# A perceptron's second product by Strassen's algorithm, in four groups of its inner dimension

## The chip, the cores and the metric

The kernel runs on one core of one Trainium2 chip. The metric is device time in microseconds for one execution of the whole program; lower is better. TensorE multiplies matrices into PSUM, which has eight banks of 128 x 512 numbers of 4 bytes here; VectorE, ScalarE and GpSimd do element by element work on SBUF and PSUM; SyncE (SP) issues transfers from DRAM.

## The reference, cut to what matters

The program is three layers over 512 tokens of width 1024: two mixer layers with a context of 256 tokens, and a third block with four mixers, a projection and a perceptron. Only the perceptron at the very end is touched. `x2` is the residual, 512 x 1024; with `h` its normalised copy and no biases:

```
hidden = square(relu(h @ w_mlp1))      # 512 x 1024 by 1024 x 4096
out    = x2 + hidden @ w_mlp2          # 512 x 4096 by 4096 x 1024
```

## The kernel before, in words

All large products are made with numbers split in two: `split` (537) casts a float32 tile to the float32r form (`hi`) and subtracts to get the rest (`lo`). `mm3` (757) then adds three matmuls in a PSUM bank: hi by hi, hi by lo, lo by hi. One matmul takes a 128 x 128 stationary operand and 512 moving columns.

Weights come in units of 128 x 1024 float32 numbers (512 KB). `wemit_raw` (719) issues the transfer of a unit into a tile `raw` on SP's queue, `wfill` (728) splits it into `whi` and `wlo` and keeps some units ahead, `wnext` (753) hands out the next one. Each filler of a list (`block2_fill`, 2496) names its units in order, so that the following stage's weights can be fetched and split during the present one.

The program is written out once in Python by a planner. Stages ("fillers") are generators that run one after another; side work is coroutines with a priority of their own, started with `spawn`. A `yield` names what the next instructions need, and `turn` (649) resumes whatever is ready by estimated times. The engine for an elementwise operation marked "*" is chosen by `best` (481): of the engines allowed, the one whose estimated queue end plus the estimated cost of this operation is earliest. The costs per column are

```
eng = (self.best(n, A=0.95, V=1.1) if self.in_psum(out, in_) else self.best(n, A=0.95, V=0.62, G=1.05)).lower()
eng = "v" if self.in_psum(out, a, b) else self.best(self.cols(out), V=1.1, G=2.0).lower()
```

for casts and for operations of two tensors (A is ScalarE, V VectorE, G GpSimd); each engine runs its instructions in the order in which they were written. SBUF tiles are placed by a plan made from their lifetimes in a first pass; `cap` (200000 bytes per partition) and `capw` (194000) limit how far ahead weights and tiles are made.

The perceptron has two rounds, each over 2048 of the 4096 hidden columns. `g_mlp1` (2321) makes 16 hidden tiles `m` of 128 columns, stored with the hidden dimension on partitions: `g_fm` (766) does 24 matmuls for a tile, ScalarE applies relu into `rl`, and a coroutine `co_hid` (2313) squares and splits it into two `hid` tiles. `g_mlp2` (2355) then makes the second product with `hid` stationary and the weights moving: for each half `c` of 512 output columns, eight weight units `u`, four token tiles `t` of 128, 6 matmuls for each (`u`, `t`), in four banks. After the last unit VectorE adds each bank to `x2` (tile name `z` in the trace); in the last round the tiles are then stored to `out`. In the last half the last two units are taken together tile by tile, so that the additions and stores spread.

Of the kernel before, what the change touches and what calls it, by code (L numbers as in the profile page):

```python
# [11 lines left out]
F32R = mybir.dt.float32r  # L12
U8 = mybir.dt.uint8
AF = mybir.ActivationFunctionType
# [4 lines left out]
D, S, CL = 1024, 512, 256  # L19
# [309 lines left out]
class Mem:  # L329
# [11 lines left out]
    def new(self, shape, dt=F32, tag="t"):  # L341
        size = int(np.prod(shape[1:])) * (1 if dt == U8 else 4)
        g = -(-size // self.G)
        i = self.plan[self.count] if self.plan is not None else (self.count * 67) % (self.n - 300)
        h = self.nc.alloc_sbuf_tensor_at(f"{tag}_{self.count}", list(shape), dt, offset=self.base + i * self.G)
        self.log.append([g, None])
        self.live += g
        self.peak = max(self.peak, self.live)
        self.curve.append((self.live, tag))
        self.count += 1  # L350
        return Tl(h, self.count - 1, g)
# [106 lines left out]
class K:  # L458
# [304 lines left out]
    def new_bank(self, n=1):  # L763
        return self.P.new(n, self.est)

    def g_fm(self, parts, evac):

        yield (self.after("h", "h0"),)
        w = self.wnext()
        hi, lo = (x.rearrange("p (k c) -> p k c", k=8) for x in w)  # L770
        yield w
        for i, (hh, hl, n) in enumerate(parts):
            yield (self.bank(), hh[:, 7], hl[:, 7])
            ps = self.new_bank()
            for k in range(8):
                self.mm3(ps[:, :n], hi[:, k], lo[:, k], hh[:, k], hl[:, k], k == 0, k == 7)
                if k % 2 and k < 7:
                    yield ()
            evac(i, ps)
            self.P.free(ps)  # L780
        self.M.free(*w)
# [158 lines left out]
    def w_ada(self, l, js, part=False):  # L940
        n = 2 if part else 4
        return [(self.I[f"wada{l}"][j * n + u], 1024, "raw") for j in js for u in range(n)]

    def w(self, name, idx):
        ap = self.I[name]
        return [(ap[i], ap.shape[2], "w") for i in idx]
# [1363 lines left out]
        for a in mix:  # L2310
            M.free(*a)

    def co_hid(self, r, hi, lo):
        M = self.M
        yield (r,)
        self.mul("*", r.f, r.f, r.f)
        yield (r,)
        self.split(hi.f, lo.f, r.f)
        M.free(r)

    def g_mlp1(self, first):
        M = self.M
        self.hid = []

        def evac(m, ps, o=0, n=S, r=None):
            r = r or M.new([128, S], tag="rl")
            self.act(r[:, o:o + n], ps[:, :n], AF.Relu)
            if o + n == S:
                hi, lo = M.new([128, S], F32R, "hid"), M.new([128, S], F32R, "hid")
                self.hid.append((hi, lo))  # L2330
                self.spawn("hid", self.co_hid(r, hi, lo), 0)
            return r
        m0 = 0
        if first:
            m0 = 3
            ws = [self.wnext() for _ in range(m0)]
            rs = {}
            for o in (0, 256):
                for t in range(o // 128, o // 128 + 2):
                    yield (self.after(("h", t)),)  # L2340
                for m in range(m0):
                    hi, lo = (x.rearrange("p (k c) -> p k c", k=8) for x in ws[m])
                    yield (hi, lo, self.bank())
                    ps = self.new_bank()
                    for k in range(8):
                        yield (self.hl[0][:, k, o:o + 256], self.hl[1][:, k, o:o + 256])
                        self.mm3(ps[:, :256], hi[:, k], lo[:, k], self.hl[0][:, k, o:o + 256], self.hl[1][:, k, o:o + 256], k == 0, k == 7)
                    rs[m] = evac(m, ps, o, 256, rs.get(m))
                    self.P.free(ps)
                    if o:  # L2350
                        M.free(*ws[m])
        for m in range(m0, 16):
            yield from self.g_fm([(self.hl[0].f, self.hl[1].f, S)], evac)

    def g_mlp2(self, last):
        nc, M, P = self.nc, self.M, self.P
        hid = self.hid
        for c in range(2):
            for _ in range(4):
                yield (self.until(lambda: self.P.used.count(False) >= 4),)  # L2360
            ps = [self.new_bank() for _ in range(4)]
            tail = 2 if last and c == 1 else 0

            def part(w, u, t):
                hi, lo = (x.rearrange("p (k c) -> p k c", k=2) for x in w)
                for kk in range(2):
                    k = 2 * u + kk
                    hh, hl = hid[k]
                    self.mm3(ps[t][:, :], hh[:, t * 128:(t + 1) * 128], hl[:, t * 128:(t + 1) * 128], hi[:, kk], lo[:, kk], k == 0, k == 15)

            def evac(t):
                x = self.x2[t][:, c * 512:(c + 1) * 512]
                self.add("v", x, x, ps[t][:, :])
                P.free(ps[t])
                if last:
                    (nc.sync if t % 2 else nc.scalar).dma_start(self.out[t * 128:(t + 1) * 128, c * 512:(c + 1) * 512], x)
            for u in range(8 - tail):
                w = self.wnext()
                if c == 0 and u == 7:
                    yield (self.after("hid"),)  # L2380
                yield (*w, hid[2 * u + 1][1])
                for t in range(4):
                    part(w, u, t)
                    yield ()
                M.free(*w)
            if tail:
                ws = [self.wnext() for _ in range(tail)]
                for t in range(4):
                    for i in range(tail):
                        part(ws[i], 8 - tail + i, t)  # L2390
                    evac(t)
                    yield ()
            else:
                for t in range(4):
                    evac(t)
        for a in hid:
            M.free(*a)

    def g_block2(self):
        M, I = self.M, self.I  # L2400
# [95 lines left out]
    def block2_fill(self):  # L2496
        w = self.w
        F = lambda name, g, u=(): Filler(name, g, u, gate=True)
        gates = []
        for m in range(8):  # L2500
            gates += w("wbr", [m]) + w("wgate", [4 * m + n for n in (0, 2, 3)])
        f = [F("block2", self.g_block2),
             F("n1", self.g_nsa_in, w("w2b", range(4)) + w("w2a", range(4))),
             F("convs", self.g_convs, w("w2f", (0, 2, 1, 3, 4, 6, 8, 5, 7, 9))),
             F("n2", self.g_nsa_in2, w("w2c", range(4)) + w("w2d", range(4))),
             F("gb", self.g_gateb, w("wgate", [4 * m + 1 for m in range(8)])),
             F("g", self.g_gates, gates),
             F("mix", self.g_mix, w("wbrb", range(2))),
             F("out2", self.g_out2, w("wout2", range(8)))]
        for r in range(2):  # L2510
            f.append(F(f"mlp{r}", lambda r=r: self.g_mlp1(r == 0), w("wm1", range(16 * r, 16 * r + 16))))
            f.append(F(f"mlp{r}o", lambda r=r: self.g_mlp2(r == 1), w("wm2", range(16 * r, 16 * r + 16))))
        return f


# [1 line left out]
           cap=200000, capw=194000, early=(0, 0),  # L2517
# [51 lines left out]
```

## Time and profile before

| | |
|---|---|
| median of 3 runs | 1953.08 us (1951.28 to 1953.52) |
| profiled execution | 1951.59 us, span 1949.9 us |
| mean granted TensorE clock | 0.982 of full speed |
| TensorE busy | 1831.2 us |
| VectorE / ScalarE / GpSimd busy | 1185.8 / 610.7 / 484.9 us |

The span runs from the first to the last instruction; the execution's own time has 1.7 us around it. TensorE matmuls are pipelined, so a matmul's own duration (389 ns for 512 columns) is longer than the distance between two of them. Almost every instruction carries line 282, that of the planner's recorder; the names of tiles tell them apart. A clock of 1.00 is 2.4 GHz and of 0.50 is 1.2 GHz.

### The profile page before, as it was taken

How to read it: one execution, taken by the hardware profiler on the slowest of the kernel's cores; microseconds unless marked ns; L12 is line 12 of the kernel's file. 1: busy time of each engine (PE TensorE's matmuls, PEld its weight loads, DVE VectorE, ACT ScalarE, POOL GpSimd, SP SyncE). 2: the span in 40 equal slices, each digit the busy share in tenths (PEclk: the TensorE clock that was granted, in tenths of full speed). 3: DMA queues.
4: the chain of work that ended last, by engine and by line, in shares of the span. 5: the costliest groups of instructions: out<-in, count | busy, mean ns of one | idle time of the engine just before them, and what ended most of it. 6: DMA issues, size and time to landing. Idle time of an engine off the chain costs nothing.

```text
span 1949.9 us, 28333 instructions
## 1 busy us (share of the span) xinstructions
PE 1831.2 (94%) x11374; PEld 1520.5 (78%) x11374; DVE 1185.8 (61%) x2072; ACT 610.7 (31%) x1281; POOL 484.9 (25%) x402
## 2 busy tenths in 40 slices
PE   6898889998999999899999899899999999999999
PEld 3688778777688788686887787778788788888887
DVE  2648686564757748766476879874632766445542
ACT  2335544553320246444152321343422211000100
POOL 1313232113422314324314453431211320000000
PEclk9999999999999999999999899999999999999999
DMA  9101001231233201003123222212232222222221
GB/s 362 66 11 45 1 12 45 88 117 68 98 119 120 95 23 38 29 12 125 47 76 132 94 87 71 71 52 70 93 100 96 98 87 87 97 98 97 84 93 61
DMA packets 45378, 159.19 MB, mean 82 GB/s; under 512 B 5040, under 2 KB 5552, under 8 KB 44992
## 3 DMA queue, kind: packets, MB, share of 16 engines
q1 hardware_dynamic: 42224, 148.54, 22.0%
q10 hardware_dynamic: 3024, 8.85, 1.2%
q8 instruction: 89, 1.46, 0.3%
q14 instruction: 41, 0.34, 0.1%
HBM read 152.12 MB, written 5.26 MB: 81 GB/s over the span
## 4 chain that ended last, share of the span: by engine, by line
PE 59%; DVE 14%; POOL 6%; issue 6%; ACT 3%; DMA 1%; SPq 0%; POOLq 0%; DVEq 0%; ACTq 0%
PE banks L282 59%; DVE cacc L282 2%; POOL t L282 2%; DVE sm L282 2%; DVE t L282 1%; DVE wlo L282 1%; ACT p L282 1%; DVE z L282 1%; POOL wlo L282 1%; DVE h L282 1%; DVE p L282 1%; DVE gt L282 1%; POOL yo L282 1%; POOL kh L282 1%; DMA raw<-win 0%
## 5 line engine op out<-in xcount | busy, mean ns | idle before, releaser
L282 PE MATMUL banks<-h,whi 128*128 128x512 f32 (+1 forms) x1968 | 578.6, 378 | 6.2 <-POOL h L282 1.9
L282 PEld LDWEIGHTS banks<-h,whi 128*128 128x128 f32 x1968 | 352.4, 191 | 69.5 <-issue 2.5
L282 PE MATMUL banks<-h,wlo 128*128 128x512 f32 (+1 forms) x984 | 367.1, 373 | 0.8 <-POOL wlo L282 0.8
L282 PE MATMUL banks<-whi,h 128*128 128x256 f32 (+3 forms) x1344 | 340.0, 335 | 15.1 <-DVE h L282 7.9
L282 DVE TENSOR_TENSOR wlo<-raw,whi 128x1024 fp32r<-128x1024 f32 (+1 forms) x169 | 223.6, 1328 | 115.5 <-PE banks L282 69.3
L282 PEld LDWEIGHTS banks<-whi,h 128*128 128x128 f32 x1344 | 237.9, 194 | 42.8 <-DVE h L282 9.5
L282 PE MATMUL banks<-wlo,h 128*128 128x256 f32 (+3 forms) x672 | 221.3, 330 | 11.0 <-DVE wlo L282 8.2
L282 POOL TENSOR_TENSOR wlo<-raw,whi 128x1024 fp32r<-128x1024 f32 (+2 forms) x47 | 116.1, 2470 | 447.9 <-DMA out<-z 299.8
L282 PEld LDWEIGHTS banks<-h,wlo 128*128 128x128 f32 x984 | 187.0, 190 | 35.7 <-issue 1.7
L282 DVE TENSOR_REDUCE sm<-banks 128x1 f32<-128x768 f32 (+5 forms) x192 | 139.8, 750 | 63.8 <-PE banks L282 61.4
L282 ACT ACTIVATE p<-banks,sm 128x768 f32<-128x768 f32 (+5 forms) x192 | 141.5, 739 | 87.7 <-DVE sm L282 68.4
L282 PE MATMUL banks<-whi,hid 128*128 128x512 f32 x512 | 157.9, 389 | 0.0
L282 ACT CAST whi<-raw 128x1024 fp32r<-128x1024 f32 (+2 forms) x94 | 93.7, 1006 | 200.6 <-PE banks L282 103.8
L282 PEld LDWEIGHTS banks<-wlo,h 128*128 128x128 f32 x672 | 130.5, 194 | 22.2 <-DVE wlo L282 9.5
L282 DVE CAST whi<-raw 128x1024 fp32r<-128x1024 f32 (+2 forms) x95 | 69.7, 740 | 104.4 <-PE banks L282 91.9
L282 ACT COPY p<-banks 128x768 f32<-128x768 f32 (+5 forms) x134 | 83.6, 632 | 94.9 <-PE banks L282 92.6
L282 PEld LDWEIGHTS banks<-whi,hid 128*128 128x128 f32 x512 | 96.1, 188 | 20.0
L282 PE MATMUL banks<-ident,p 128*128 128x128 f32 x656 | 96.8, 277 | 6.5 <-ACT p L282 2.4
L282 PE MATMUL banks<-wlo,hid 128*128 128x512 f32 x256 | 99.6, 389 | 0.0
L282 POOL TENSOR_TENSOR t<-t,mhalf 128x1 f32<-128x1 f32 (+5 forms) x51 | 60.6, 1189 | 142.8 <-DVE t L282 136.7
L282 PEld LDWEIGHTS banks<-ident,p 128*128 128x128 f32 x656 | 73.9, 141 | 23.5 <-ACT p L282 6.1
L282 ACT ACTIVATE rl<-banks 128x512 f32<-128x512 f32 (+1 forms) x35 | 19.7, 562 | 177.7 <-PE banks L282 177.7
(339 smaller groups left out, 2829.1 us busy)
## 6 DMA issues: line engine op xcount, KB each, us to landing
raw<-wm SPq DMA_DIRECT2D x64, 512.0 KB, 3.5
raw<-win SPq DMA_DIRECT2D x60, 512.0 KB, 3.6
raw<-wada SPq DMA_DIRECT2D x48, 512.0 KB, 4.9
raw<-wgate SPq DMA_DIRECT2D x32, 512.0 KB, 3.5
raw<-wout SPq DMA_DIRECT2D x24, 512.0 KB, 3.9
raw<-w2f SPq DMA_DIRECT2D x10, 512.0 KB, 3.4
xr<-xtok SPq DMA_DIRECT2D x6, 512.0 KB, 3.5
x<-z SPq DMA_DIRECT2D x6, 512.0 KB, 4.8
```

The lines of the kernel that those rows point to most:

```text
L282: return f(*a, **kw)
```

## The change

The inner dimension of the second product, 4096, is taken in four groups of 1024 instead of two of 2048; the filler list has four pairs of stages, and the first product's columns are handed out so that neighbouring hidden tiles belong to the two halves of a group. In a group the hidden matrix (512 tokens x 1024) and the weights (1024 x 1024) are each cut into four quarters. Strassen's algorithm in Winograd's form makes the 2 x 2 block product from seven products of quarters, numbered in four rounds: product 0 has two of them (`a11` by `b11`, `a12` by `b21`), 1 has two, 2 has two, 3 has one.

`co_hid` now takes two hidden tiles, squares them, forms four sums of quarters of 256 tokens in `hs`, and splits seven quarters into `hid`. `mlp2_prep` fetches two to four raw weight quarters for a step, forms the sums that the step's product needs (none, two, three, none), and splits the one or two operands. Since sums are formed anew in each round, quarters of weights are fetched more than once: 20 units for a group where it was 8. `g_mlp2` runs eight steps (product, half of its inner dimension) in the order of `MLP2`. At the top of a step it prepares further steps until three are ready, but only while no `hid` coroutine is alive and memory is below a limit, or if none is ready. Each step holds 24 matmuls (12 for product 3). After the second half of a product, `evac` adds its banks to `x2`, product 0's and 1's through a tile `mu`. The first two steps' operands are prepared by `g_mlp1` after its sixth and seventh tile, for which it takes its last three weight units early.

```diff
     def new_bank(self, n=1):
-    def g_fm(self, parts, evac):
+    def g_fm(self, parts, evac, w=None):
-        w = self.wnext()
+        w = w or self.wnext()
...
     def w_ada(self, l, js, part=False):
+    def w_mlp2(self, r):
+        q = lambda i, j, u: self.w("wm2", [16 * (r // 2) + 8 * j + 4 * (r % 2) + 2 * i + u])[0][:2] + ("raw",)
+        rounds = ((0, 0), (1, 0)), ((0, 1), (1, 1), (0, 0)), ((0, 0), (0, 1), (1, 1), (1, 0)), ((1, 1),)
+        return [q(i, j, u) for p, u in self.MLP2 for i, j in rounds[p]]
     def w(self, name, idx):
...
-    def co_hid(self, r, hi, lo):
+    def co_hid(self, k, r0, r1):
-        yield (r,)
-        self.mul("*", r.f, r.f, r.f)
-        yield (r,)
-        self.split(hi.f, lo.f, r.f)
-        M.free(r)
+        new = lambda n=2: (M.new([128, n, 256], F32R, "hid"), M.new([128, n, 256], F32R, "hid"))
+        yield (r0, r1)
+        self.mul("*", r0.f, r0.f, r0.f)
+        self.mul("*", r1.f, r1.f, r1.f)
+        yield (r0, r1)
+        a11, a21, a12, a22 = r0[:, 0:256], r0[:, 256:512], r1[:, 0:256], r1[:, 256:512]
+        put = lambda o, i, x: self.split(o[0][:, i], o[1][:, i], x)
+        oa = new()
+        put(oa, 0, a11)
+        put(oa, 1, a12)
+        self.hid[0, k] = oa
+        t = M.new([128, 4, 256], tag="hs")
+        self.add("*", t[:, 2], a21, a22)
+        self.sub("*", t[:, 1], a11, a21)
+        yield (t,)
+        self.sub("*", t[:, 0], t[:, 2], a11)
+        yield (t,)
+        self.sub("*", t[:, 3], a12, t[:, 0])
+        oc = new()
+        put(oc, 0, t[:, 2])
+        put(oc, 1, a22)
+        self.hid[2, k] = oc
+        M.free(r0, r1)
+        yield (t,)
+        ob, od = new(), new(1)
+        self.split(ob[0].f, ob[1].f, t[:, 0:2])
+        put(od, 0, t[:, 3])
+        self.hid[1, k], self.hid[3, k] = ob, od
+        M.free(t)
     def g_mlp1(self, first):
-        self.hid = []
+        self.hid = {}
+        half = []
         def evac(m, ps, o=0, n=S, r=None):
-                hi, lo = M.new([128, S], F32R, "hid"), M.new([128, S], F32R, "hid")
-                self.hid.append((hi, lo))
-                self.spawn("hid", self.co_hid(r, hi, lo), 0)
+                half.append(r)
+                if len(half) % 2 == 0:
+                    self.spawn("hid", self.co_hid(len(half) // 2 - 1, *half[-2:]), 0)
...
-        for m in range(m0, 16):
+        for m in range(m0, 5):
+        ws = [self.wnext() for _ in range(3)]
+        self.pre = []
+        for m in range(3):
+            yield from self.g_fm([(self.hl[0].f, self.hl[1].f, S)], evac, ws[m])
+            if m < 2:
+                self.pre.append(self.mlp2_prep(m))
+    MLP2 = (0, 0), (1, 0), (0, 1), (1, 1), (2, 0), (2, 1), (3, 0), (3, 1)
+    def mlp2_prep(self, p):
+        M = self.M
+        ws = []
+        for _ in range((2, 3, 4, 1)[p]):
+            self.wfill(1, 4)
+            ws.append(self.wrdy.pop(0)[0])
+        if p == 1:
+            b12, b22, b11 = ws
+            self.sub("*", b12.f, b22.f, b12.f)
+            self.add("*", b11.f, b12.f, b11.f)
+            M.free(b22)
+            ops = [b11, b12]
+        elif p == 2:
+            b11, b12, b22, b21 = ws
+            self.sub("*", b21.f, b22.f, b21.f)
+            self.sub("*", b12.f, b12.f, b11.f)
+            self.sub("*", b21.f, b21.f, b12.f)
+            M.free(b11, b22)
+            ops = [b12, b21]
+        else:
+            ops = ws
+        out = []
+        for x in ops:
+            hi, lo = M.new([128, 1024], F32R, "whi"), M.new([128, 1024], F32R, "wlo")
+            self.split(hi.f, lo.f, x.f)
+            M.free(x)
+            out.append((hi, lo))
+        return out
     def g_mlp2(self, last):
         nc, M, P = self.nc, self.M, self.P
...
+        hid, x2 = self.hid, self.x2
+        steps = self.MLP2
+        ready, ps, U, nprep = self.pre, {}, {}, 2
+        C = lambda i, c: x2[i][:, c * 512:(c + 1) * 512]
+        def out(i, c):
+            if last:
+                (nc.sync if i % 2 else nc.scalar).dma_start(self.out[i * 128:(i + 1) * 128, c * 512:(c + 1) * 512], C(i, c))
+        def evac(p, t):
+            a = ps[p, 0, t]
+            b = ps.get((p, 1, t))
+            if p == 0:
+                u = U[t] = M.new([128, 512], tag="mu")
+                self.act(u.f, a[:, :], AF.Copy)
+                self.add("v", C(t, 0), C(t, 0), b[:, :])
+                self.add("*", C(t, 0), C(t, 0), u.f)
+                out(t, 0)
+            elif p == 1:
+                u = U[t]
+                self.add("v", u.f, u.f, a[:, :])
+                self.add("*", C(t, 1), C(t, 1), u.f)
+                v = M.new([128, 512], tag="mu")
+                self.add("v", v.f, u.f, b[:, :])
+                M.free(u)
+                for c in range(2):
+                    self.add("*", C(2 + t, c), C(2 + t, c), v.f)
+                M.free(v)
+            elif p == 2:
+                self.sub("v", C(2 + t, 0), C(2 + t, 0), b[:, :])
+                self.add("v", C(2 + t, 1), C(2 + t, 1), a[:, :])
+                self.add("v", C(t, 1), C(t, 1), a[:, :])
+                out(2 + t, 0)
+                out(2 + t, 1)
+            else:
+                self.add("v", C(t, 1), C(t, 1), a[:, :])
+                out(t, 1)
+            P.free(a)
+            if b is not None:
+                P.free(b)
+        for p, u in steps:
+            while nprep < 8 and len(ready) < 3 and (not ready or (not any(a.key == "hid" for a in self.acts) and M.live * Mem.G + 24000 <= self.cfg["cap"])):
+                ready.append(self.mlp2_prep(steps[nprep][0]))
+                nprep += 1
+            if nprep == 8 and not last:
+                self.wfill(2, 3)
+            n = 1 if p == 3 else 2
+            if u == 0:
+                for _ in range(4):
+                    yield (self.until(lambda: P.used.count(False) >= 2 * n),)
+                for j in range(n):
+                    for t in range(2):
+                        ps[p, j, t] = self.new_bank()
+            w = ready.pop(0)
+            yield (self.until(lambda: (p, 2 * u + 1) in hid),)
+            yield tuple(x for y in w for x in y) + hid[p, 2 * u + 1]
+            for t in range(2):
+                for j in range(n):
+                    hi, lo = (x.rearrange("p (k c) -> p k c", k=2) for x in w[j])
+                    for kk in range(2):
+                        k = 2 * u + kk
+                        hh, hl = hid[p, k]
+                        r = slice(t * 128, (t + 1) * 128)
+                        self.mm3(ps[p, j, t][:, :], hh[:, j, r], hl[:, j, r], hi[:, kk], lo[:, kk], k == 0, k == 3)
                     yield ()
...
+                if u == 1:
+                    evac(p, t)
+            for x in w:
+                M.free(*x)
+            for kk in range(2):
+                M.free(*hid[p, 2 * u + kk])
...
-        for r in range(2):
-            f.append(F(f"mlp{r}", lambda r=r: self.g_mlp1(r == 0), w("wm1", range(16 * r, 16 * r + 16))))
-            f.append(F(f"mlp{r}o", lambda r=r: self.g_mlp2(r == 1), w("wm2", range(16 * r, 16 * r + 16))))
+        for r in range(4):
+            f.append(F(f"mlp{r}", lambda r=r: self.g_mlp1(r == 0), w("wm1", [8 * r + 4 * (i % 2) + i // 2 for i in range(8)])))
+            f.append(F(f"mlp{r}o", lambda r=r: self.g_mlp2(r == 3), self.w_mlp2(r)))
```

## Rows read from the trace of the kernel before

**Rows 1.** The page, part 1: busy time, share of the span, instructions.
```profile
PE 1831.2 (94%) x11374; PEld 1520.5 (78%) x11374; DVE 1185.8 (61%) x2072; ACT 610.7 (31%) x1281; POOL 484.9 (25%) x402
```

**Rows 2.** Chain that ended last, from 1560: start, us, what.
```profile
1604.48 341.68 PE banks L282 x1532
...
1946.19 0.69 DVE z L282
```

**Rows 3.** Windows: us; PE, PEld, DVE, ACT, POOL busy (instructions); PEclk, DMA share, GB/s.
```profile
1684.60:1772.00 87.40, 87.40 (x387) 72.38 (x387) 40.94 (x47) 2.71 (x3) 0.00 (x0) 1.00 0.37 122
1772.00:1859.00 87.00, 87.00 (x386) 72.06 (x385) 49.69 (x71) 8.99 (x15) 0.00 (x0) 1.00 0.21 71
```

**Rows 4.** Timeline of VectorE, two places: start, us, instruction.
```profile
1727.23 0.69 DVE L282 TENSOR_TENSOR z<-z,banks 128x512 f32<-128x512 f32 x1 [0.67 <-PE banks L282]
1728.59 0.69 DVE L282 TENSOR_TENSOR z<-z,banks 128x512 f32<-128x512 f32 x1 [0.67 <-PE banks L282]
...
1768.79 1.22 DVE L282 TENSOR_TENSOR wlo<-raw,whi 128x1024 fp32r<-128x1024 f32 x1
1769.92 0.68 DVE L282 TENSOR_TENSOR z<-z,banks 128x512 f32<-128x512 f32 x1
1770.52 0.69 DVE L282 CAST whi<-raw 128x1024 fp32r<-128x1024 f32 x1
1771.12 0.68 DVE L282 TENSOR_TENSOR z<-z,banks 128x512 f32<-128x512 f32 x1
```

**Rows 5.** Timeline of VectorE, narrower operations.
```profile
1293.00 0.41 DVE L282 TENSOR_TENSOR stk<-banks,stk 128x256 fp32r<-128x256 f32 x1
1293.34 0.27 DVE L282 TENSOR_REDUCE sm<-banks 128x1 f32<-128x128 f32 x1
...
1644.47 0.42 DVE L282 CAST hid<-rl 128x512 fp32r<-128x512 f32 x1
1644.92 0.69 DVE L282 TENSOR_TENSOR hid<-rl,hid 128x512 fp32r<-128x512 f32 x1
```

**Rows 6.** Groups by form, whole span; the last from 1575 on: busy, mean ns.
```profile
L282 POOL TENSOR_TENSOR wlo<-raw,whi 128x1024 fp32r<-128x1024 f32 x38 | 96.3, 2535 | 416.9 <-DMA out<-z 299.8 <-DVE whi L282 76.3 <-ACT whi L282 16.9
L282 POOL TENSOR_TENSOR h<-h,ab 128x512 f32<-128x512 f32 x12 | 14.1, 1176 | 24.3 <-DVE h L282 24.3
L282 DVE TENSOR_TENSOR wlo<-raw,whi 128x1024 fp32r<-128x1024 f32 x154 | 207.5, 1352 | 109.7 <-PE banks L282 67.3 <-ACT whi L282 29.5 <-issue 8.0
L282 ACT CAST whi<-raw 128x1024 fp32r<-128x1024 f32 x76 | 78.9, 1047 | 174.2 <-PE banks L282 100.8 <-DVE wlo L282 37.3 <-DMA raw<-wgate 14.2
L282 DVE TENSOR_TENSOR wlo<-raw,whi 128x1024 fp32r<-128x1024 f32 x59 | 72.1, 1224 | 48.7 <-PE banks L282 36.8 <-ACT whi L282 10.3 <-DVE whi L282 0.5
```

**Rows 7.** Timelines: GpSimd alone, then GpSimd with VectorE and TensorE.
```profile
1288.49 2.39 POOL L282 TENSOR_TENSOR wlo<-raw,whi 128x1024 fp32r<-128x1024 f32 x1 [5.69 <-DVE stk L282]
...
1539.99 2.79 POOL L282 TENSOR_TENSOR wlo<-raw,whi 128x1024 fp32r<-128x1024 f32 x1
1540.50 2.82 DVE L282 TENSOR_TENSOR gt<-gt,gt 128x512 f32<-128x512 f32 x1
1542.83 0.50 PE L282 MATMUL banks<-wlo,mix 128*128 128x512 f32 x1 [2.19 <-POOL wlo L282]
```

**Rows 8.** Windows of 1 us around that pause, columns as in rows 3.
```profile
1541.00:1542.00 1.00, 0.00 (x0) 0.00 (x0) 1.00 (x1) 0.00 (x0) 1.00 (x1) 1.00 0.99 406
1543.00:1544.00 1.00, 1.00 (x4) 0.76 (x5) 1.00 (x3) 0.63 (x1) 0.00 (x0) 0.65 0.05 21
1544.00:1545.00 1.00, 1.00 (x4) 0.81 (x3) 1.00 (x2) 0.00 (x0) 0.99 (x1) 0.50 0.00 0
...
1546.00:1547.00 1.00, 1.00 (x3) 0.69 (x3) 1.00 (x3) 0.53 (x1) 0.00 (x0) 0.64 0.00 0
```

**Rows 9.** DMA issues (KB, us to landing), and SP's waits from 1600 on.
```profile
raw<-wm SPq DMA_DIRECT2D x64, 512.0 KB, 3.5
...
SPq L282 <- DVE wlo L282: 140.5, 32, 10.1
```

More of the change, by code (lines that the diff above doesn't have):

```diff
@@ L2355, in g_mlp2 @@
     def g_mlp2(self, last):
         nc, M, P = self.nc, self.M, self.P
[L2357 to L2383, printed above, removed]
-                    yield ()
[L2385 to L2395, printed above, removed]
@@ L2396, in g_mlp2 @@
-        for a in hid:
-            M.free(*a)
+        hid, x2 = self.hid, self.x2
[36 more added lines that the diff above has]
+                P.free(b)
```

## The prediction, made before the changed kernel was run

> **What bounds the kernel now.** I read the engine totals first: TensorE is busy 94% of the span, VectorE 61%, ScalarE 31%, GpSimd 25% [rows 1]. That is an average, so next comes the chain that ended last, for the perceptron alone: from 1604.5 us to 1946.2 us it is one unbroken piece of TensorE, and after it only a 0.7 us addition and the last store remain [rows 2]. The windows then show what is idle meanwhile: in the 87 us of one quarter of the perceptron VectorE is busy 50 us where it falls mostly on the first product and 41 us on the second, ScalarE 3 to 9 us, GpSimd nothing, at full clock [rows 3]. So in this stage TensorE alone sets the time, and any matmul less is time won as long as the other three keep up.
>
> The profiled execution took 1951.6 us and the median of the runs shown is 1953.1 us; I sum against the first and add 1.5 us at the end. A difference under 0.2% (4 us) is about what a measurement of this kernel can't tell from no change.
>
> **What the change removes.** Two additions that each close six matmuls of a tile start 1.36 us apart [rows 4], so a matmul costs TensorE 0.2267 us, and 24 of them 5.44 us. The second product is 768 matmuls before (2 groups x 2 halves x 16 slices x 4 tiles x 3). After, each of the four groups has 7 products x 4 slices x 2 tiles x 3 = 168, in all 672. 96 x 0.2267 = 21.8 us go, 5.44 us for each group; their weight loads go with them. A group becomes 192 + 168 = 360 matmuls, 81.6 us, against 87.0.
>
> **What it adds.** I price the other engines' work by start-to-start times in a full queue: on VectorE 0.60 us for an addition of 512 columns, 1.13 for a two-tensor operation of 1024, 0.60 for a cast of 1024 [rows 4]; 0.34 for 256 columns, 0.45 for a cast of 512 [rows 5]. GpSimd needs 2.4 us without disturbance for 1024 (2.54 mean) and 1.18 for 512, ScalarE 1.05 for a cast [rows 6, 7]. A group then holds, if all is put on VectorE:
> - weights of the first product, 8 splits (cast and subtraction, 1.73): 13.8, as before
> - weights of the second, 14 splits where there were 8: 24.2, and 10 sums of 1024 columns: 11.3
> - the hidden tiles, for each of 4 pairs 2 squares, 4 sums, 5 casts and 5 subtractions of 256, one of each of 512: 7.0 a pair, 28.0 (before, by the same prices, 3.3 and 13.2)
> - draining PSUM and combining: 14 additions that read PSUM and 8 that don't, 13.2 (before 4 additions, 2.4).
>
> That is 90 us for 81.6 us of TensorE. So it can't all stay on VectorE; `best` (481) will send casts to ScalarE, which has room, and two-tensor operations to GpSimd.
>
> **Where it falls.** Each group takes these steps: (0,0), (1,0), (0,1), (1,1), (2,0), (2,1), 5.44 us each, and (3,0), (3,1), 2.72 us each. Two preparations are made during the first product. The next ones may be written only when no `hid` coroutine is alive, unless nothing is ready. The last pair's coroutine starts with step 1 and holds 7 us of queue work in rounds that wait for each other, longer than that step; so at step 2 nothing is prepared, and at step 3 the list is empty and the operands are made while TensorE waits: two casts and two subtractions, of which the second pair goes partly to ScalarE and GpSimd, 1.05 + 2.4, or serially 3.46 on VectorE. I take 3.5 us.
>
> From there to the start of step 8 TensorE needs 4 x 5.44 + 2.72 = 24.5 us. The queue must by then have finished the preparations of steps 3 to 8 (3.46, 5.72, 6.85, 6.85, 1.73, 1.73) and, between them, the drains of products 0 and 1 (2.4 and 6.0): 34.7 us on one engine. Behind these wait product 2's and 3's matmuls, which need both the operands and the banks; and as VectorE's queue runs in order, a subtraction that waits for ScalarE's cast also holds the drains behind it. With 7 of the 10 casts on the idle ScalarE 30.5 remain. This is 6.0 us over, the first wait of 3.5 included.
>
> **What GpSimd takes off is the disputed price.** The nearest row: at 1540.50 a VectorE two-tensor operation of 512 columns took 2.82 us instead of 0.68; a GpSimd one of 1024 had begun at 1539.99 and ended at 1542.78, and VectorE's ended 0.54 us later, its own 0.60 [rows 7]. The matmuls behind them waited 2.19 us. So an operation that GpSimd takes costs VectorE not nothing but GpSimd's own 2.4 us. The Trainium skill, SBUF — State Buffer, section "Who interferes with whom", states this as a lock: a VectorE instruction with two SBUF inputs, or in a two-port mode, and a GpSimd instruction that reads SBUF exclude each other for the whole instruction. The trace agrees in that row. By that rule GpSimd's help costs time and the sum is the +17 below; without it, with the mean slowing alone (1.35 us for a subtraction over the whole kernel, 1.22 where GpSimd is idle [rows 6]), it would be the -8 of the first rival.
>
> Over the whole kernel GpSimd took 38 of the 192 weight subtractions of 1024 columns [rows 6], one in five. Of the 18 two-tensor operations of 1024 and 8 of 512 in this stretch that is 3.6 and 1.6, each dearer by 1.26 and 0.58: +5.4; the six additions from PSUM can run beside GpSimd, and I credit half of their 3.6: -1.8. So 34.1 us, 9.6 over 24.5. Per group 9.6 - 5.4 = +4.2, four groups **+17 us**. Bounds: no use of GpSimd +0.6 a group, +2; one in three under exclusion +7.9 a group, +31; below, free help -8, and with no waits at all -21.8.
>
> The rest I put at nothing, with its cover: 20 weight transfers of 512 KB a group where 8 were, with the first product's 28 x 0.524 MB in 82 us, 179 GB/s, against 406 in a burst [rows 8]; each lands 3.5 us after its issue [rows 9] and up to four are ahead. The stores of the last group follow their additions as before. Work outside the perceptron is the same, though the memory plan may place it otherwise.
>
> **The clock.** After a pause of 2.19 us the granted clock fell to 0.65, twice 0.50 (one of the two rows is shown), and 0.64 in four successive microseconds, down to 1.2 GHz [rows 7, 8]: 1.7 us lost. Where the queue is the bound this is hidden, since the matmuls slow down while they would wait anyway; where it isn't, each long pause costs 1.7 us more.
>
> **Rivals.**
> - *Faster.* GpSimd and VectorE share the work without much loss, or the hidden tiles are done before step 2 and the preparations stay three ahead. Then 22 us of VectorE work fit into 24.5, and only the wait at step 3 is left or not even it: -8 to -21.8, centre **1939**. For it: VectorE idles 46 us in a quarter now [rows 3], ScalarE nearly always. Against: the row at 1540.50, and that work of one step arrives in bursts. It decides as soon as waits stay under 5.44 us a group.
> - *No change.* Only the wait at step 3 happens, 3.5 us, and its clock drop, 1.7: 5.2 against 5.44, -1 in all, **1952**. Here a GpSimd that is used little also ends (+2).
> - *Much slower.* SP issues weight loads in order and already waits 140 us for VectorE's subtractions to free buffers [rows 9]. If both preparations of product 2, four transfers each, start a landing of 3.5 us late, 28 us come on top: **1998**.
> - That the matmuls don't go, or cost more, I exclude: form and 512 columns stay.
>
> **Numbers.** Chances: forecast 0.50 (1951.6 + 17 + 1.5 = 1970; its own range 1958 to 1987), faster 0.34, no change 0.12, much slower 0.04. The range runs from the middle of the faster case to the upper bound with something over it, 1936 to 1992. Of the forecast 0.04 lies within 0.2%, and of the no-change case 0.02 on either side: faster 0.36, same 0.12, slower 0.52.
>
> **What would show it.** Right: 672 matmuls of the second product; TensorE idle for several us at each group's third step and again at the fifth to seventh, released by `wlo` and `z` or `mu`; GpSimd busy with subtractions of 1024 columns; VectorE near full in those 40 us; a clock under 1.0 there. Wrong: a perceptron still unbroken in the chain, or operands ready before each step, or VectorE's subtractions at 1.22 us beside a busy GpSimd, or SP's transfers as what was waited for.

## The result, and the profile after

The changed kernel takes 2008.6 us (median of 4 runs, 2005.23 to 2010.48) against 1953.28: the ratio is 1.0285, 95% interval 1.0272 to 1.0298. It is slower, as forecast, but by 55 us where 17 were forecast and 39 was the upper end. The profiled execution took 2005.23 us.

The page, engine totals after:

```profile
span 2003.5 us, 28787 instructions
...
PE 1834.9 (92%) x11278; PEld 1518.8 (76%) x11278; DVE 1367.3 (68%) x2238; ACT 661.0 (33%) x1355; POOL 683.3 (34%) x522
```

Against [rows 1] TensorE has 96 matmuls less, as the change says, and VectorE (DVE) 182 us and GpSimd (POOL) 198 us more. The tile `hid` after, TensorE's matmuls (count, duration, first and last start): 448 + 224 = 672 of the second product, from 1656.9 us on.

```profile
L282 PE MATMUL banks<-whi,hid x448: 387/389/797, 1656.9 to 1999.3; 128*128 128x512 f32 x150
...
L282 PE MATMUL banks<-wlo,hid x224: 387/389/796, 1657.2 to 1999.1; 128*128 128x512 f32 x112
```

Windows of the changed kernel, one for each of four stages (columns as in rows 3); the second is the first product of group 2, the others are the seven products of groups 1, 2 and 3:

```profile
1656.90:1709.70 52.80, 43.48 (x169) 34.41 (x168) 47.38 (x43) 10.63 (x13) 30.75 (x15) 0.87 0.45 157
1709.70:1753.20 43.50, 43.50 (x193) 36.04 (x192) 42.54 (x56) 7.38 (x14) 16.93 (x15) 1.00 0.43 149
1753.20:1805.10 51.90, 40.35 (x170) 32.58 (x169) 50.46 (x45) 10.61 (x13) 32.90 (x16) 0.90 0.54 192
...
1848.60:1903.30 54.70, 41.20 (x169) 32.92 (x168) 52.30 (x47) 10.68 (x13) 37.12 (x18) 0.88 0.48 173
```

The first product runs unbroken, 43.5 us. The seven products take 52.8, 51.9, 54.7 and 52.9 us (the fourth not shown) where 168 matmuls need 38.1: 60 us lost in four groups, against 21.8 us won. For 42 of the 60 TensorE stood; the other 18 are matmuls that ran slower, at a mean clock of 0.87 to 0.90. Added up, VectorE and GpSimd are busy 78 to 89 us in each of these stages of 52 to 55.

A timeline of the third step of group 2, TensorE, VectorE and GpSimd (in brackets how long the engine was idle before, and what released it):

```profile
1770.82 0.80 PE L282 MATMUL banks<-whi,hid 128*128 128x512 f32 x1 [5.19 <-POOL whi L282]
1777.98 0.79 PE L282 MATMUL banks<-wlo,hid 128*128 128x512 f32 x1 [6.37 <-DVE wlo L282]
...
1771.35 6.58 DVE L282 TENSOR_TENSOR wlo<-raw,whi 128x1024 fp32r<-128x1024 f32 x2
...
1771.22 5.62 POOL L282 TENSOR_TENSOR raw<-raw,raw 128x1024 f32<-128x1024 f32 x2 [0.45 <-DMA raw<-wm]
1776.81 3.35 POOL L282 TENSOR_TENSOR wlo<-raw,whi 128x1024 fp32r<-128x1024 f32 x1
```

TensorE stands 5.19 and then 6.37 us, 11.6 of the 13.8 us that this group lost. Meanwhile VectorE needs 6.58 us for two subtractions that take 1.13 us each, start to start, in [rows 4], and GpSimd's two sums lie in the same 6 us. The groups by form from 1575 us on (busy, mean ns) say the same of the whole perceptron: 1.58 and 1.65 us on VectorE for what took 1.22 in [rows 6], 2.85 and 2.77 us on GpSimd, which took 41 of the 127 operations of this width.

```profile
L282 DVE TENSOR_TENSOR wlo<-raw,whi 128x1024 fp32r<-128x1024 f32 x58 | 90.9, 1579 | 1.9 <-POOL whi L282 0.9 <-POOL hid L282 0.6
...
L282 POOL TENSOR_TENSOR wlo<-raw,whi 128x1024 fp32r<-128x1024 f32 x29 | 82.5, 2850 | 10.1 <-ACT whi L282 6.4 <-DVE whi L282 2.9 <-DMA raw<-wm 0.7
L282 DVE TENSOR_TENSOR raw<-raw,raw 128x1024 f32<-128x1024 f32 x28 | 45.9, 1646 | 10.1 <-DMA raw<-wm 6.3 <-POOL raw L282 2.3 <-issue 1.1
...
L282 POOL TENSOR_TENSOR raw<-raw,raw 128x1024 f32<-128x1024 f32 x12 | 33.2, 2770 | 15.9 <-DMA raw<-wm 15.7
```

One part of the loss lies where nothing was edited. The first relu of the perceptron (tile `rl`, ScalarE; first and last start) comes at 1594.2 us in the kernel before,

```profile
L282 ACT ACTIVATE rl<-banks x35: 364/598/602, 1594.2 to 1859.2; 128x512 f32<-128x512 f32 x29, 128x256 f32<-128x256 f32 x6
```

and at 1607.4 in the changed one:

```profile
L282 ACT ACTIVATE rl<-banks x35: 377/592/601, 1607.4 to 1947.0; 128x512 f32<-128x512 f32 x29, 128x256 f32<-128x256 f32 x6
```

So of the 53.6 us between the spans 13.2 were lost ahead of the perceptron and 40.4 in it.

### The profile page after: what moved, and what is told of

Same layout as the page of the kernel before. It is cut to its first block, busy times and chain, and to the rows that moved or that the text cites. A ratio compares the mean times of both kernels' runs of the same rounds, so it can differ in the third digit from the quotient of the medians.

```text
span 2003.5 us, 28787 instructions
## 1 busy us (share of the span) xinstructions
PE 1834.9 (92%) x11278; PEld 1518.8 (76%) x11278; DVE 1367.3 (68%) x2238; ACT 661.0 (33%) x1355; POOL 683.3 (34%) x522
## 5 line engine op out<-in xcount | busy, mean ns | idle before, releaser
L282 PE MATMUL banks<-whi,h 128*128 128x256 f32 (+3 forms) x1344 | 343.0, 337 | 13.2 <-DVE h L282 8.1
L282 DVE TENSOR_TENSOR wlo<-raw,whi 128x1024 fp32r<-128x1024 f32 (+1 forms) x167 | 229.1, 1380 | 66.3 <-ACT whi L282 29.9
L282 POOL TENSOR_TENSOR wlo<-raw,whi 128x1024 fp32r<-128x1024 f32 (+2 forms) x73 | 187.9, 2577 | 145.7 <-DVE whi L282 67.6
L282 ACT CAST whi<-raw 128x1024 fp32r<-128x1024 f32 (+2 forms) x125 | 126.1, 1018 | 194.7 <-PE banks L282 58.5
L282 PE MATMUL banks<-whi,hid 128*128 128x512 f32 x448 | 149.6, 414 | 16.7 <-POOL whi L282 12.5
L282 PEld LDWEIGHTS banks<-whi,hid 128*128 128x128 f32 x448 | 90.3, 202 | 38.1 <-POOL whi L282 13.8
L282 PE MATMUL banks<-wlo,hid 128*128 128x512 f32 x224 | 93.6, 418 | 25.6 <-DVE wlo L282 23.7
L282 POOL TENSOR_SCALAR whi<-raw 128x1024 fp32r<-128x1024 f32 (+1 forms) x39 | 46.6, 1196 | 173.2 <-PE banks L282 56.2
L282 POOL TENSOR_TENSOR gt<-gt,gt 128x512 f32<-128x512 f32 x20 | 31.2, 1562 | 135.4 <-DVE gt L282 130.4
```

The costliest lines, as they stand in the source:

```text
L282: return f(*a, **kw)
```

## The experiments

Two theories: the loss in the perceptron is VectorE and GpSimd excluding each other; the loss ahead of it is the new memory plan, since the plan is made for the whole program at once. Rivals: the order in which the planner writes the preparations, GpSimd as a slow link in a chain (its own longer operations are waited for), an overloaded VectorE, the regrouping itself.

**Two swaps of the memory plan.** `FIXED` is a list of 1569 offsets, those of the other kernel's tiles up to the perceptron; the tiles behind them are fitted as before.

```diff
+        nf = len(FIXED)
-        order = sorted(range(n), key=
+        order = list(range(nf)) + sorted(range(nf, n), key=
...
         for c, i in enumerate(order):
             d = done[:c]
+            if i < nf:
+                at[i], done[c] = FIXED[i], i
+                continue
```

> The changed kernel, with the tiles made ahead of the perceptron put where the kernel before has them. Theory (13 us of the loss come from the new memory plan of the untouched stages): the perceptron's first relu starts near 1594 us instead of 1607, and the time is about 1995 us. Rival (the loss ahead of the perceptron comes from something else, such as the weights' order or a disturbed run): the first relu stays near 1607 and the time near 2008.

x_plan took 1990.64 us (ratio to the kernel before 1.0187, interval 1.0166 to 1.0207; the figures in brackets below are the same two), its first relu:

```profile
L282 ACT ACTIVATE rl<-banks x35: 364/594/600, 1594.0 to 1931.6; 128x512 f32<-128x512 f32 x29, 128x256 f32<-128x256 f32 x6
```

> The kernel before, with the tiles made ahead of the perceptron put where the changed kernel has them. Theory (memory plan): about 1966 us, 13 us over the kernel before, all of it ahead of the perceptron. Rival (the plan is innocent): 1953 us.

b_plan took 1969.9 us (1.0072, 1.0054 to 1.0090):

```profile
L282 ACT ACTIVATE rl<-banks x35: 378/598/602, 1615.7 to 1878.6; 128x512 f32<-128x512 f32 x29, 128x256 f32<-128x256 f32 x6
```

The plan alone moves the first relu from 1607.4 to 1594.0 in the one kernel and from 1594.2 to 1615.7 in the other. What it does shows in the waits up to 1580 us (total us, times, longest). Before:

```profile
SPq L282 <- POOL wlo L282: 21.4, 4, 8.5
...
PE banks L282 <- DVE wlo L282: 9.4, 6, 2.7
```

With the changed kernel's plan, b_plan:

```profile
SPq L282 <- POOL wlo L282: 121.7, 12, 33.6
...
PE banks L282 <- DVE wlo L282: 19.7, 9, 5.0
```

Weight loads wait longer for a buffer that GpSimd still reads, and TensorE waits 10 us more for split weights. That these waits are the 16 us of the time was not tried by itself.

A plan also carries an order with it. Of TensorE's first 9700 matmuls, all ahead of the perceptron, 381 places differ between the kernel before and the changed one, named by their tiles; none differ between the kernel before and x_plan, nor between the changed kernel and b_plan. So a swap changes both where tiles lie and the order in which the engines run, and which of the two costs the time is open.

In the perceptron x_plan does the same operations on the same engines as the changed kernel, form by form, and still waits elsewhere. TensorE's waits in its second product add up to 35.9 us, against 42 in the changed kernel, and only 2.8 of them fall in the third step, against 36.5. Most, 24 us, come in the fifth, where TensorE waits for banks to be drained (`z`, `mu`). The two longest of group 1:

```profile
1664.93 0.49 PE L282 MATMUL banks<-whi,hid 128*128 128x512 f32 x1 [2.99 <-ACT mu L282]
...
1674.82 0.79 PE L282 MATMUL banks<-whi,hid 128*128 128x512 f32 x1 [6.04 <-DVE z L282]
```

**GpSimd closed in the perceptron.** x_nog is x_plan with

```diff
+    def gp(self, c):
+        return {} if self.nog else dict(G=c)
...
-            eng = "v" if self.in_psum(out, a, b) else self.best(self.cols(out), V=1.1, G=2.0).lower()
+            eng = "v" if self.in_psum(out, a, b) else self.best(self.cols(out), V=1.1, **self.gp(2.0)).lower()
```

the same for casts, and `self.nog = True` at the start of `g_mlp1`.

> As x_plan, and in the perceptron no elementwise work goes to GpSimd; VectorE and ScalarE take it. Theory (VectorE and GpSimd exclude each other, so GpSimd's 2.4 us cost more than VectorE's 1.1): the seven-product stages fall from 53 to about 45 us each, in all about 32 us less than x_plan, near 1963 us. Rival (GpSimd's help is real and VectorE alone is overloaded, 90 us of work for 81.6 of TensorE): slower than x_plan, by up to 39 us, near 2034 us.

Measured 1935.05 us, 0.9897 (0.9883 to 0.9912): 56 us less than x_plan and 1.0% less than the kernel before. Windows of the seven products of groups 1 and 2 in x_nog:

```profile
1645.60:1683.70 38.10, 38.10 (x169) 31.53 (x169) 36.23 (x50) 15.45 (x20) 0.00 (x0) 1.00 0.62 223
...
1727.20:1765.40 38.20, 38.20 (x170) 31.49 (x169) 33.83 (x44) 14.50 (x18) 0.00 (x0) 1.00 0.63 207
```

TensorE never stops in them. VectorE, now alone, is *less* busy than with help: 36 and 34 us against 47 and 50. From 1600 us on its subtractions are short again:

```profile
L282 DVE TENSOR_TENSOR wlo<-raw,whi 128x1024 fp32r<-128x1024 f32 x80 | 95.6, 1216 | 3.9 <-ACT whi L282 3.7
```

**The written order.** x_gate takes one condition out of x_plan:

```diff
-            while nprep < 8 and len(ready) < 3 and (not ready or (not any(a.key == "hid" for a in self.acts) and M.live * Mem.G + 24000 <= self.cfg["cap"])):
+            while nprep < 8 and len(ready) < 3 and (not ready or (M.live * Mem.G + 24000 <= self.cfg["cap"])):
```

> As x_plan, but steps may be prepared while a hidden tile is still being made, so step 3 finds its operands written one step earlier. Theory (the sum of the work of VectorE and GpSimd is the bound, the written order only says where the wait falls): the waits move to the steps behind, and the time stays within 12 us of x_plan. Rival (late writing at step 3 is the loss itself): the waits of 11 us a group go, about 40 us less than x_plan, near 1955 us.

Measured 1998.68 us (1.0222, 1.0205 to 1.0239), 8 us over x_plan: the waits move and do not go, 44.5 us in the second product against 35.9. In TensorE's timeline the longest now stands at the hidden tiles:

```profile
1677.29 0.80 PE L282 MATMUL banks<-whi,hid 128*128 128x512 f32 x1 [10.16 <-ACT hid L282]
```

The "11 us a group" of the rival are those of the changed kernel; x_plan, from which x_gate starts, has 2.8 us in the third step in all, so x_gate could not win 40 us there. Against the rival stands x_plan itself: the same operations under the same condition, nearly no wait in the third step, and still 36 us over the kernel before.

**GpSimd work that nobody waits for.** nog_read and nog_write add to x_nog a scratch tile and, at each prepared operand, the lines shown (the planner does not time them):

```diff
+                self.nc.real.gpsimd.tensor_tensor(self.scr.f, self.scr.f, self.scr.f, op=ALU.add)
```
```diff
+                for _ in range(2):
+                    self.nc.real.gpsimd.memset(self.scr.f, 0.0)
```

> x_nog with idle work added: for each of the 56 operands prepared, one GpSimd addition of 128 x 1024 on a scratch tile that nothing else reads (written order as in x_nog). Theory (exclusion): about 2.4 us of each is lost to VectorE, 34 us a group on top of some 75 of 82; the seven-product stages grow by 10 to 27 us each, the time is 1975 to 2040 us and VectorE's subtractions get longer than 1.22 us. Rival (GpSimd hurt only as a slow link in the chain of a step's operands): nobody waits for this work, so 1935 us as x_nog.

> As nog_read, but each addition is replaced by two fills of the same scratch tile, which write SBUF and read nothing. If GpSimd excludes VectorE's two-tensor operations only while it reads SBUF: close to x_nog, 1935 to 1945 us, casts alone getting longer. If any GpSimd work on SBUF excludes VectorE: as nog_read.

Since nothing holds this work back, it did not spread over the groups: GpSimd ran all of it at the perceptron's start, 56 additions in 130 us, or 112 fills in 121. That makes the test sharper. nog_read took 2014.54 us (1.0320, 1.0305 to 1.0336), nog_write 1934.32 (0.9910, 0.9895 to 0.9924). The window of the additions in nog_read, and two groups of VectorE's operations in it:

```profile
1592.60:1720.40 127.80, 64.54 (x320) 53.69 (x319) 122.87 (x68) 17.47 (x34) 123.67 (x57) 0.75 0.14 50
...
L282 DVE TENSOR_TENSOR wlo<-raw,whi 128x1024 fp32r<-128x1024 f32 x7 | 19.5, 2816 | 0.0
...
L282 DVE TENSOR_TENSOR h<-banks,vec 128x512 f32<-128x512 f32 x6 | 3.9, 678 | 0.1
```

The same in nog_write, with its casts:

```profile
1592.60:1709.00 116.40, 113.54 (x567) 96.61 (x566) 102.75 (x153) 39.77 (x64) 110.13 (x112) 0.99 0.45 155
...
L282 DVE TENSOR_TENSOR wlo<-raw,whi 128x1024 fp32r<-128x1024 f32 x26 | 30.9, 1215 | 2.0 <-ACT whi L282 1.4 <-PE banks L282 0.5
...
L282 DVE CAST whi<-raw 128x1024 fp32r<-128x1024 f32 x7 | 7.6, 1112 | 0.0
```

In both GpSimd is busy nearly without a break. Where it reads SBUF, VectorE finishes 68 instructions in 128 us and a subtraction takes 2.82 us; where it only writes, 153 in 116 us, 1.22 us each. An operation with one input in PSUM (`h<-banks,vec`) keeps its 0.68 us beside the reads too. Beside the fills only casts and one scaling (`xn`, 0.75 to 1.42 us) grow; the cast of a weight unit takes 1.11 us, against 0.68 in x_nog over the same stretch:

```profile
L282 DVE CAST whi<-raw 128x1024 fp32r<-128x1024 f32 x9 | 6.1, 684 | 0.0
```

Nobody waits for these additions, and they cost 80 us against nog_write: the exclusion costs time without any slow link. How much of the changed kernel's own loss is GpSimd as a slow link was not separated; operations on GpSimd ended 14.3 of its 42 us of waits, those on VectorE 24.9.

**The regrouping alone.** b_four is the kernel before, with `range(4)` groups of 8 hidden tiles and four weight units for each half, eight products as they were.

> The kernel before with its second product in four groups of 1024 and the eight products as they were: the regrouping alone, no Strassen, tiles ahead of the perceptron placed as before. Theory (regrouping costs only 16 more additions, hidden behind TensorE): 1953 to 1956 us. Rival (shorter stages alone bring waits): 1960 us or more.

Measured 1953.26 us (1.0004, 0.9992 to 1.0016): the regrouping costs nothing.

**The changed kernel with GpSimd closed and no other edit.**

> The changed kernel with the perceptron's work kept off GpSimd and nothing else changed, so with a memory plan of its own. Theory (two separate causes that add up: exclusion in the perceptron, plan ahead of it): the perceptron as in x_nog, the stages ahead of it 0 to 20 us later than before by the new plan: 1935 to 1955 us.

Measured 1938.5 us (0.9933, 0.9917 to 0.9950). Its own plan, fitted to other lifetimes again, puts the first relu at 1600.9 us.

**How far it carries.** nog_mix closes GpSimd from `g_mix` on (1533 fixed offsets), nog_all in the whole program with a plan of its own; b_nog_all is the kernel before, closed in the whole program. Work that the program gives to GpSimd by name stays there, 93 us in nog_all.

> As x_nog, with GpSimd closed to chosen work already from the block's last mixing stage on, where the row at 1540.50 us of the kernel before shows one exclusion with a pause of 2.19 us and 1.7 us of low clock. Theory (exclusion costs there too): 2 to 5 us less than x_nog, 1930 to 1933 us. Rival (that place has slack): 1935 us.

> The changed kernel with GpSimd closed to chosen work in the whole program, memory plan of its own. If exclusion makes GpSimd's help a loss everywhere: 1900 to 1930 us. If it pays where VectorE has gaps or reads PSUM, as in the attention stages: 1940 us or more.

> The kernel before (eight products, two groups) with GpSimd closed to casts and two-tensor operations in the whole program, as in nog_all. If the gain of nog_all is the exclusion alone, and the seven products add their 21.8 us on top only because VectorE is free of GpSimd: 1870 to 1880 us, 16 to 26 us over nog_all's 1854. If the seven products need more than is hidden: within 10 us of nog_all.

> nog_all beside b_nog_all on one chip, for their difference: 1854 us.

nog_mix took 1922.62 us (0.9839, 0.9821 to 0.9858), a larger gain than expected. nog_all took 1854.44 (0.9505, 0.9481 to 0.9528), beyond the best that was expected, and b_nog_all 1876.43 (0.9610, 0.9594 to 0.9626) beside 1855.93 of nog_all_again (0.9508, 0.9486 to 0.9529). The page of nog_all:

```profile
PE 1798.9 (97%) x11278; PEld 1496.4 (80%) x11278; DVE 1334.8 (72%) x2509; ACT 750.1 (40%) x1502; POOL 93.3 (5%) x104
```

So the seven products are worth 1876.43 - 1855.93 = 20.5 us when GpSimd stays out, near their 21.8, and keeping GpSimd out is worth 77 us to the kernel before (1953.42 in the same session). The plan differs between these kernels too; how much of the 77 us and of the 20.5 is the plan's was not separated. The figure with the plan kept is that of x_nog: 19.3 us less than the kernel before, whose GpSimd works 2.4 us in the perceptron.

## Why the prediction was right or wrong

Right: the direction, the gain and the exclusion. There are 672 matmuls, 0.2267 us each, an unbroken first product, a clock under 1.0 in the seven-product stages and a VectorE that is nearly full there. x_nog's stages of 38.1 us show the gain of 21.8 us, and nog_read shows the exclusion.

Wrong, a size: the queue from the third step on. It was put at 34.1 us for 24.5, 9.6 lost a group; measured are 60 / 4 = 15.0. The term that was too small is GpSimd's share. I took one operation in five from the whole kernel. In the perceptron it was 41 of the 127 operations of 1024 columns, one in three, for which the prediction gives +31 us as its upper bound, and the perceptron lost 40.4. In the four seven-product stages alone it was 30 of 76, 7.5 a group where the sum has 3.6, and 3 additions of 512 columns where it has 1.6. Group 2, where GpSimd has 8 of 20:

```profile
L282 POOL TENSOR_TENSOR wlo<-raw,whi 128x1024 fp32r<-128x1024 f32 x6 | 17.5, 2924 | 0.0
L282 DVE TENSOR_TENSOR wlo<-raw,whi 128x1024 fp32r<-128x1024 f32 x7 | 16.4, 2351 | 0.1
L282 DVE TENSOR_TENSOR raw<-raw,raw 128x1024 f32<-128x1024 f32 x5 | 8.3, 1656 | 1.2 <-issue 1.1
L282 POOL TENSOR_TENSOR raw<-raw,raw 128x1024 f32<-128x1024 f32 x2 | 5.5, 2748 | 0.6 <-DMA raw<-wm 0.5
```

With these counts and the prediction's own prices the queue is 30.5 + 7.5 x 1.26 + 3 x 0.58 - 1.8 = 39.9 us, 15.4 over 24.5, or about +40 us for four groups. So the price that was read off the row at 1540.50 us [rows 7] holds. That the sum meets the 15.0 so closely is in part luck, since the time was not lost where the sum has it (below).

Wrong, a step: "Work outside the perceptron is the same, though the memory plan may place it otherwise" was put at nothing. It cost 13.2 us. x_plan and b_plan show that this comes with the plan, in both directions. With it and the +40 the sum would have been 1951.6 + 40 + 13 + 1.5 = 2006 us, against 2008.6. With the plan kept (x_plan, 1990.64 us) the time lies just inside the range, 36 us over the kernel before where 17 were forecast.

Wrong, the place and its reason. The third step was to wait 3.5 us because its preparations were written too late, and the rest was to come in the fifth to seventh step, in part for `z` or `mu`. The changed kernel waits 9.1 us a group in the third step and 1.4 behind it, always for `whi` or `wlo` and never for `z` or `mu`; x_plan waits mostly in the fifth step for `z` and `mu`, as the prediction has it, and hardly in the third. x_nog has the same condition and no wait. VectorE may run ahead of TensorE as far as its data and buffers let it: in x_nog the first cast and the two subtractions behind the hidden tiles' work end at 1738.0 us, and TensorE goes into its third step 10.9 us after 1727.24, at 1738.1, without a pause.

```profile
1734.81 0.68 DVE L282 CAST whi<-raw 128x1024 fp32r<-128x1024 f32 x1
1735.53 2.48 DVE L282 TENSOR_TENSOR wlo<-raw,whi 128x1024 fp32r<-128x1024 f32 x2
```

In the changed kernel's group 2 the same cast begins 16.6 us into the stage, where it is 7.6 in x_nog, and the two subtractions end at 24.7 us, where it is 10.8:

```profile
1769.79 1.53 DVE L282 CAST whi<-raw 128x1024 fp32r<-128x1024 f32 x1
```

So the third step waits there because the queues are behind by then. For the same reason the bound "no use of GpSimd, +2" was wrong: the measured effect of that case, against the kernel before, is -19 us with the plan kept. The bound put 7 of 10 casts on ScalarE and took a wait that did not come; x_nog's VectorE has 34 to 36 us of work in 38.

Wrong, a smaller term: the low clock was to be hidden behind the queue. Where no wait follows it is not: after its last pause, which ends at 1777.98, group 2 needs 27.1 us for 113 matmuls that take 25.6 at full clock. Over the four groups such ends cost 8.4 us.

The rivals: the faster case names preparations that stay ahead, and its 1939 lies near x_nog's 1935, by luck, since its condition was a GpSimd that helps without much loss, and in x_nog GpSimd does not help at all. Late weight loads (1998) are not needed to explain the loss: x_nog moves the same weights at 207 to 223 GB/s in the stages shown with no wait, and none of the changed kernel's waits in the second product was released by a transfer.

## What to carry to other kernels

When two engines exclude each other, help is not free: price an operation that reads SBUF and is moved to GpSimd at GpSimd's own duration for both engines, as long as VectorE's queue holds operations on two SBUF tensors, and let a planner that balances queues know it. Take the share that is moved from the stage at hand and not from the whole kernel. An idea that saves matmuls by elementwise work may fail on where that work is put and not on its amount; test the placement before dropping the idea. And where one memory plan serves a whole program, hold it fixed when you compare two versions of one stage: here the plan, with the order that comes with it, was worth 18 us to the changed kernel and 16 to the kernel before, most of the gain that was looked for.

## What the runs showed of the hardware that was not expected

GpSimd that reads SBUF stretches VectorE's operation on two SBUF tensors from 1.22 to 2.82 us when it runs without a break, and GpSimd that only writes leaves it at 1.22 and stretches casts, 0.68 to 1.11 us, and a scaling. The Trainium skill, SBUF — State Buffer, section "Who interferes with whom", draws the same line, between GpSimd's reads for two-input operations and all of its work for the two-port modes; the runs agree with the first half, and with the second in that casts and a scaling grew beside GpSimd's writes, though no run shows in which mode these ran. New was the size: with GpSimd kept off the shared work the kernel before took 3.9% less (1876.43 against 1953.42 us), its memory plan being refitted with it.
